# Layer norm and GELU: variance + eps and -mean/sigma of each tile computed on GpSimd instead of VectorE

## Chip, cores, metric

One core of one Trainium2 chip runs the kernel. The metric is device time in microseconds (us). The record calls a run slow when it is over 1.5% above the fastest of its kernel.

## The reference

```python
x: (8, 1024, 2048) float32; gamma, beta: (2048,); eps = 1e-5
mean = np.mean(x, axis=-1, keepdims=True)
var = np.var(x, axis=-1, keepdims=True)
out = gamma * (x - mean) / np.sqrt(var + eps) + beta
return 0.5 * out * (1 + np.tanh(np.sqrt(2 / np.pi) * (out + 0.044715 * out ** 3)))
```

## The kernel before

There are 8192 rows. A tile is 128 rows of 2048 columns; a batch is four tiles, moved by one load and one store of 4 MB. Five batch buffers are used in turn, and a load waits until the store from its buffer has landed. The last batch is cut into smaller pieces, so there are 65 tiles in all, and the stores are 15 large ones and a few small ones.

Each tile passes through four engines. VectorE takes statistics (four instructions of 512 columns and an aggregation) and adds eps to the variance. GpSimd computes (var + eps)^-0.5, which is 1/sigma; the text calls it the power. VectorE makes -mean/sigma of it. ScalarE scales (`yk = x/sigma - mean/sigma`, in bf16). VectorE multiplies by gamma (`zg`). TensorE adds beta and `zg` in PSUM. ScalarE applies GELU and, after each fourth tile, issues the store. In the code and the views, `sts` and `mvs` are the statistics and their aggregation (mean and variance), `ves` is variance + eps, `rss` 1/sigma and `nms` -mean/sigma. DVE stands for VectorE, ACT for ScalarE, POOL for GpSimd, PE for TensorE, and ACTq for what ScalarE's sequencer does itself, such as issuing a store. The parts that the change touches (`...` marks what is left out):

```python
            @block.gpsimd
            def _(po):
                ...
                def power(t, count):
                    c = slice(t % R, t % R + 1)
                    po.tensor_tensor(out=rss[:, c], in0=ves[:, c], in1=mhalf,
                                     op=ALU.pow)._wait_ge(s_a, count).then_inc(s_q, 1)
                ...
            @block.vector
            def _(ve):
                def mean(q, count):
                    c = slice(q, q + 1)
                    ve.tensor_scalar(out=nms[:, c], in0=mvs[:, q, 0:1], scalar1=rss[:, c], scalar2=-1.0,
                                     op0=ALU.mult, op1=ALU.mult)._wait_ge(s_q, count).then_inc(s_p, 1)

                def step(x, q, wait, count, before, count_q, count_n):
                    xr = x.rearrange("p (s f) -> p s f", f=FMAX)
                    for j in range(nsub):
                        ins = ve.bn_stats(out=sts[:, q, j, :], in_=xr[:, j, :])
                        if j == 0:
                            ...                               # the wait for the load
                            if before is not None:
                                mean(before, count_q)         # -mean/sigma of the tile before
                    ins.then_inc(s_o, 1)
                    ve.bn_aggr(out=mvs[:, q], in_=sts[:, q])._wait_ge(s_o, count + 1).then_inc(s_o, 1)
                    ve.tensor_scalar(out=ves[:, q:q + 1], in0=mvs[:, q, 1:2], scalar1=float(eps), scalar2=1.0,
                                     op0=ALU.add, op1=ALU.mult)._wait_ge(s_o, count + 2).then_inc(s_a, 1)
                    if count_n:
                        scale(before, count_n)

                def scale(q, count):                          # the gamma multiplication
                    ve.tensor_tensor(out=zgs[q % 2], in0=yks[q % 2], in1=g_t,
                                     op=ALU.mult)._wait_ge(s_n, count).then_inc(s_z, 1)
                ...
            @block.scalar
            def _(ac):
                ...
                for t in range(n_t + 1):
                    if t < n_t:
                        c = slice(t % R, t % R + 1)
                        ac.activation(out=yks[t % 2], in_=tiles[t], func=ACT.Identity, scale=rss[:, c],
                                      bias=nms[:, c])._wait_ge(s_p, t + 1).then_inc(s_n, 1)
                    i = t - 1
                    ...
                    ins = ac.activation(out=tiles[i], in_=pss[i % 2], func=ACT.Gelu_apprx_tanh)._wait_ge(s_t, i + 1)
                    ...                                       # the store, after each fourth tile
```

Of the kernel before, what the change touches and what calls it, by code (L numbers as in the profile page):

```python
# [8 lines left out]
ALU = mybir.AluOpType  # L9

R = 4
SLOTS = 5
# [6 lines left out]
def kernel(  # L19
# [41 lines left out]
    def sb(name, shape, dt):  # L61
        return pool.tile(shape, dt, name=name)

    xts = [sb(f"xt{s}", [P, R, d], f32) for s in range(SLOTS)]
# [11 lines left out]
    sts = sb("sts", [P, R, nsub, nc.vector.BN_STATS_DIM], f32)  # L76
    mvs = sb("mvs", [P, R, 2], f32)
    ves = sb("ves", [P, R], f32)
    rss = sb("rss", [P, R], f32)
    nms = sb("nms", [P, R], f32)  # L80

    def sem(name):
        return tc.alloc_semaphore(name)

    s_first = [sem(f"first{q}") for q in range(R)]
    s_tail = sem("tail")
    s_load_h = sem("load_h")
# [6 lines left out]
    s_o = sem("o")  # L94
    s_a = sem("a")
    s_z = sem("z")
    s_q = sem("q")
    s_p = sem("p")
# [7 lines left out]
    def slot(b):  # L106
        return (b + SLOTS - 1) % SLOTS

    def row(p):
        return rows[p:p + 1, :, :d // K]  # L110

    def split(v):
        return v.rearrange("o (k f) -> o k f", k=K)
# [11 lines left out]
    tiles = [xts[slot(b)][:, q] for b in range(B) for q in range(R)] + [xts[slot(B)][:, 0]]  # L125
    n_t = len(tiles)
# [9 lines left out]
    with tc.tile_critical(no_gpsimd_drain=True):  # L136
        with nc.Block(no_gpsimd_drain=True) as block:

            @block.sync
            def _(sy):  # L140
                for b in range(B):
                    s = slot(b)
                    if stored(b):
                        sy.wait_ge(s_store[s], stored(b))
                    for q in range(R):
                        if b == 0:
                            sy.dma_start(out=xts[s][:, q:q + 1], in_=xg[0, :, q:q + 1]).then_inc(s_first[q], 16)
                    if 0 < b < B - 1:
                        sy.dma_start(out=xts[s], in_=xg[b]).then_inc(s_load[s], 16)
                        if s == slot(B - 1):  # L150
                            sy.sem_inc(s_tail, 32)
                sy.dma_start(out=x_end[:, :R - 1], in_=last(xf)).then_inc(s_load[slot(B - 1)], 16)
                for v, a in x_half[:2]:
                    sy.dma_start(out=a, in_=v).then_inc(s_tail, 16)
                sy.wait_ge(s_store[slot(B)], stored(B))
                sy.dma_start(out=x_half[2][1], in_=x_half[2][0]).then_inc(s_load_h, 16)

            @block.gpsimd
            def _(po):
                po.memset(ones, 1.0)  # L160
                po.memset(ones_b, 1.0)
                po.memset(mhalf, -0.5)
                po.memset(ident, 0.0).then_inc(s_setp, 1)
                po.affine_select(out=ident, in_=ident, compare_op=ALU.not_equal, fill=1.0, base=0,  # L164
                                 pattern=[[-1, P]], channel_multiplier=1)._wait_ge(s_setp, 1).then_inc(s_setp, 1)

                def power(t, count):
                    c = slice(t % R, t % R + 1)
                    po.tensor_tensor(out=rss[:, c], in0=ves[:, c], in1=mhalf,  # L169
                                     op=ALU.pow)._wait_ge(s_a, count).then_inc(s_q, 1)  # L170

                with po.Fori(0, B):
                    for k in range(R):
                        power(k, k + 1)
                    po.sem_inc(s_a, -R)
                power(n_t - 1, 1)

            @block.vector
            def _(ve):
                def mean(q, count):  # L180

                    c = slice(q, q + 1)
                    ve.tensor_scalar(out=nms[:, c], in0=mvs[:, q, 0:1], scalar1=rss[:, c], scalar2=-1.0,  # L183
                                     op0=ALU.mult, op1=ALU.mult)._wait_ge(s_q, count).then_inc(s_p, 1)

                def step(x, q, wait, count, before, count_q, count_n):

                    xr = x.rearrange("p (s f) -> p s f", f=FMAX)
                    for j in range(nsub):
                        ins = ve.bn_stats(out=sts[:, q, j, :], in_=xr[:, j, :])  # L190
                        if j == 0:
                            if wait:
                                ins._wait_ge(*wait)
                                if wait[0] not in s_first:
                                    ins.then_inc(wait[0], -wait[1])
                            if before is not None:
                                mean(before, count_q)
                    ins.then_inc(s_o, 1)
                    ve.bn_aggr(out=mvs[:, q], in_=sts[:, q])._wait_ge(s_o, count + 1).then_inc(s_o, 1)  # L199
                    ve.tensor_scalar(out=ves[:, q:q + 1], in0=mvs[:, q, 1:2], scalar1=float(eps), scalar2=1.0,  # L200
                                     op0=ALU.add, op1=ALU.mult)._wait_ge(s_o, count + 2).then_inc(s_a, 1)
                    if count_n:
                        scale(before, count_n)

                def scale(q, count):
                    ve.tensor_tensor(out=zgs[q % 2], in0=yks[q % 2], in1=g_t,  # L206
                                     op=ALU.mult)._wait_ge(s_n, count).then_inc(s_z, 1)

                ve.memset(b_hl, 0.0).then_inc(s_m, 1)  # L209
                for q in range(R):  # L210
                    step(tiles[q], q, (s_first[q], 16), 2 * q, q - 1 if q else None, q, q)
                    if q == 0:

                        ve.tensor_tensor(out=split(b_hl[32:33]), in0=row(32), in1=split(b_hl[32:33]),  # L214
                                         op=ALU.subtract)._wait_ge(s_c, 2).then_inc(s_m, 1)
                        ve.wait_ge(s_c, 3)
                ve.sem_inc(s_o, -2 * R)
                ve.sem_inc(s_q, -(R - 1))
                ve.sem_inc(s_n, -(R - 1))
                with ve.Fori(0, (B - 1) // SLOTS):  # L220
                    for k in range(SLOTS * R):
                        s, q = divmod(k, R)
                        wait = (s_load[s], 16) if q == 0 else (s_tail, 32) if (s, q) == (slot(B - 1), R - 1) else None
                        step(xts[s][:, q], q, wait, 2 * k, (q - 1) % R, k + 1, k + 1)
                    ve.sem_inc(s_o, -2 * SLOTS * R)
                    ve.sem_inc(s_q, -SLOTS * R)
                    ve.sem_inc(s_n, -SLOTS * R)
                step(tiles[-1], 0, (s_load_h, 16), 0, R - 1, 1, 1)
                mean(0, 2)
                scale(0, 2)  # L230

            @block.scalar
# [104 lines left out]
```

## Time and profile before

| | before |
|---|---|
| time, median | 319.69 us (319.66 to 320.07) |
| busy: VectorE / ScalarE / TensorE / GpSimd | 269.2 / 257.7 / 248.0 / 79.5 us |
| the 16 DMA engines | 90% or more busy in 38 of 40 slices, 422 GB/s over the span |
| one store to the next, early / late | 16.69 / 19.36 us |

A busy share is an average over the whole span, so it can be high on an engine that bounds nothing. Three views are needed here: the slices (is anything busy all the time?), a table by stretch (does the same work take different times in different stretches?), and the waits (what did the busiest engine wait for when it did wait?). The prediction below shows the lines of all three.

### The profile page before, as it was taken

The page shows a single profiled execution, that of the slowest core. Times are in us where ns is not written, and L with a number is a line of the kernel's source. Part 1 is how long each engine was busy: PE and PEld are TensorE (multiplying, and loading weights), DVE is VectorE, ACT ScalarE, POOL GpSimd, SP SyncE. Part 2 cuts the span into 40 slices and gives each one's busy share as a digit, 9 for nine tenths or more (in the row PEclk, how much of TensorE's full clock was granted, in tenths as well). Part 3 has the DMA queues.
Part 4 walks back from the last instruction along what each step waited for, and adds up shares of the span by engine and source line. Part 5 has one row for each costly group of instructions (what it writes and reads, how often), then busy time and mean ns, then how long its engine had stood idle before and what let it go on. Part 6 is the DMA issues. An engine that isn't in the chain of part 4 may idle for free.

```text
span 317.9 us, 2115 instructions
## 1 busy us (share of the span) xinstructions
PE 248.0 (78%) x528; PEld 58.1 (18%) x528; DVE 269.2 (85%) x522; ACT 257.7 (81%) x134; POOL 79.5 (25%) x74
## 2 busy tenths in 40 slices
PE   2769988888888898888877868688685995898840
PEld 1211222111212122211211111121121121122100
DVE  3499999999999999999969789696996969999610
ACT  3579999999999999998969879697896959998850
POOL 1033323232323231323213212232213213221100
DMA  7999999999999999999999999999999999999994
GB/s 287 442 458 400 455 400 421 437 449 412 454 404 455 413 449 433 425 445 412 445 421 445 437 425 449 408 449 412 454 433 429 445 431 409 446 424 430 437 408 206
DMA packets 5753, 134.27 MB, mean 422 GB/s; under 512 B 710, under 2 KB 758, under 8 KB 758
## 3 DMA queue, kind: packets, MB, share of 16 engines
q1 hardware_dynamic: 2899, 67.11, 49.4%
q10 hardware_dynamic: 2851, 67.13, 49.0%
q14 instruction: 3, 0.02, 0.0%
HBM read 67.13 MB, written 67.11 MB: 422 GB/s over the span
## 4 chain that ended last, share of the span: by engine, by line
DMA 43%; DVE 27%; ACT 21%; PE 2%; issue 2%; ACTq 2%; DVEq 0%; SPq 0%
DMA out_dram<-xt 26%; DVE sts L190 15%; DMA xt<-in_x_dram 15%; ACT yk L246 13%; ACT xt L251 8%; DVE zg L206 8%; PE ps L269 2%; DMA rows<-in_gamma_dram 2%; DVE mvs L199 2%; ACTq L256 2%; DVE nms L183 1%; DVE ves L200 1%; ACT g_t L241 1%; ACTq L260 0%; DVEq L220 0%
## 5 line engine op out<-in xcount | busy, mean ns | idle before, releaser
L190 DVE BATCH_NORM_STATS2 sts<-xt 128x6 f32<-128x512 f32 x260 | 165.9, 679 | 22.1 <-DMA xt<-in_x_dram 19.8
L246 ACT ACTIVATE yk<-xt,nms,rss 128x2048 bf16<-128x2048 f32 x65 | 136.1, 2093 | 40.4 <-DVE nms L183 39.9
L286 PE MATMUL ps<-zg,ident 128*128 128x512 bf16 x260 | 122.7, 627 | 49.6 <-DVE zg L206 49.6
L169 POOL TENSOR_TENSOR rss<-ves,mhalf 128x1 f32<-128x1 f32 x65 | 78.5, 1208 | 218.5 <-DVE ves L200 159.0
L282 PE MATMUL ps<-b_hl,ones_b 33*128 33x512 bf16 x260 | 122.5, 624 | 2.2 <-PEq L277 2.2
L251 ACT ACTIVATE xt<-ps 128x2048 f32<-128x2048 f32 x65 | 120.6, 1856 | 1.6 <-PE ps L286 1.6
L206 DVE TENSOR_TENSOR zg<-yk,g_t 128x2048 bf16<-128x2048 bf16 x65 | 79.2, 1219 | 5.0 <-ACT yk L246 3.0
L286 PEld LDWEIGHTS ps<-zg,ident 128*128 128x128 bf16 x260 | 28.1, 130 | 144.2 <-DVE zg L206 108.4
L282 PEld LDWEIGHTS ps<-b_hl,ones_b 33*128 33x128 bf16 x260 | 27.5, 127 | 93.5 <-issue 89.8
L199 DVE BATCH_NORM_AGGREGATE mvs<-sts 128x2 f32<-128x24 f32 x65 | 17.1, 263 | 2.2
L183 DVE TENSOR_SCALAR nms<-mvs,rss 128x1 f32<-128x1 f32 x65 | 12.7, 196 | 0.0
L269 PE MATMUL ps<-rows,ones 1*128 1x512 f32 x8 | 7.2, 1076 | 6.1 <-DMA rows<-in_gamma_dram 6.1
L200 DVE TENSOR_SCALAR ves<-mvs 128x1 f32<-128x1 f32 x65 | 10.0, 153 | 2.2
L238 ACT ACTIVATE b_hl<-rows 1x2048 bf16<-1x2048 f32 x1 | 1.9, 1910 | 4.6 <-DMA rows<-in_beta_dram 4.6
L269 PEld LDWEIGHTS ps<-rows,ones 1*128 1x128 f32 x8 | 2.5, 325 | 9.2 <-DMA rows<-in_gamma_dram 6.1
L241 ACT ACTIVATE g_t<-ps 128x2048 bf16<-128x2048 f32 x1 | 1.9, 1877 | 2.6 <-PE ps L269 2.6
L214 DVE TENSOR_TENSOR b_hl<-rows,b_hl 1x2048 bf16<-1x2048 f32 x1 | 2.3, 2281 | 1.9 <-ACT b_hl L239 1.9
L234 ACT ACT_TABLE_LOAD x1 | 1.3, 1283 | 0.9 <-SPq L136 0.9
L209 DVE MEMSET b_hl<- 33x1024 uint32 x1 | 0.9, 912 | 1.2 <-SPq L136 1.2
L239 ACT ACTIVATE b_hl<-rows 1x2048 bf16<-1x2048 f32 x1 | 1.9, 1909 | 0.0
L160 POOL MEMSET ones<- 65x128 f32 x1 | 0.2, 201 | 0.5 <-SPq L136 0.5
L164 POOL TENSOR_SCALAR_AFFINE_SELECT ident<-ident 128x128 bf16<-128x128 bf16 x1 | 0.3, 292 | 0.1
(7 smaller groups left out, 0.9 us busy)
## 6 DMA issues: line engine op xcount, KB each, us to landing
out_dram<-xt ACTq DMA_DIRECT2D x15, 4096.0 KB, 35.0
xt<-in_x_dram SPq DMA_DIRECT2D x14, 4096.0 KB, 26.4
xt<-in_x_dram SPq DMA_DIRECT2D x4, 1024.0 KB, 8.2
xt<-in_x_dram SPq DMA_DIRECT2D x1, 3072.0 KB, 23.0
out_dram<-xt ACTq DMA_DIRECT2D x3, 1024.0 KB
xt<-in_x_dram SPq DMA_DIRECT2D x1, 512.0 KB, 21.4
out_dram<-xt ACTq DMA_DIRECT2D x1, 512.0 KB, 8.7
xt<-in_x_dram SPq DMA_DIRECT2D x1, 480.0 KB
```

The lines of the kernel that those rows point to most:

```text
L169: po.tensor_tensor(out=rss[:, c], in0=ves[:, c], in1=mhalf, op=ALU.pow)._wait_ge(s_a, count).then_inc(s_q, 1)
L183: ve.tensor_scalar(out=nms[:, c], in0=mvs[:, q, 0:1], scalar1=rss[:, c], scalar2=-1.0, op0=ALU.mult, op1=ALU.mult)._wait_ge(s_q, count).th ...
L190: ins = ve.bn_stats(out=sts[:, q, j, :], in_=xr[:, j, :])
L199: ve.bn_aggr(out=mvs[:, q], in_=sts[:, q])._wait_ge(s_o, count + 1).then_inc(s_o, 1)
L200: ve.tensor_scalar(out=ves[:, q:q + 1], in0=mvs[:, q, 1:2], scalar1=float(eps), scalar2=1.0, op0=ALU.add, op1=ALU.mult)._wait_ge(s_o, coun ...
L206: ve.tensor_tensor(out=zgs[q % 2], in0=yks[q % 2], in1=g_t, op=ALU.mult)._wait_ge(s_n, count).then_inc(s_z, 1)
L246: ac.activation(out=yks[t % 2], in_=tiles[t], func=ACT.Identity, scale=rss[:, c], bias=nms[:, c])._wait_ge(s_p, t + 1).then_inc(s_n, 1)
L251: ins = ac.activation(out=tiles[i], in_=pss[i % 2], func=ACT.Gelu_apprx_tanh)._wait_ge(s_t, i + 1)
L256: dma = ac.dma_start(out=v, in_=a)
L269: ins = pe.matmul(pss[0][:, cols(j)], lhsT=ones[64:65], rhs=rows[64:65, j * K // nsub:(j + 1) * K // nsub, :d // K], start=True, stop=True)
L282: ins = pe.matmul(ps[:, cols(j)], lhsT=ones_b, rhs=b_hl[:, cols(j)], start=True, stop=False)
L286: ins = pe.matmul(ps[:, cols(j)], lhsT=ident, rhs=zg[:, cols(j)], start=False, stop=True)
```

## The change

The intent: VectorE is the busiest engine, and -mean/sigma of a tile stood in VectorE's queue behind the first statistics of the next tile. GpSimd has both inputs and idles three quarters of the time, so it takes over both small instructions, and VectorE keeps six for each tile.

```diff
-                def power(t, count):
-                    c = slice(t % R, t % R + 1)
+                def small(t, k):
+                    q = t % R
+                    c = slice(q, q + 1)
+                    po.tensor_scalar(out=ves[:, c], in0=mvs[:, q, 1:2], scalar1=float(eps), scalar2=1.0,
+                                     op0=ALU.add, op1=ALU.mult)._wait_ge(s_a, k + 1).then_inc(s_q, 1)
                     po.tensor_tensor(out=rss[:, c], in0=ves[:, c], in1=mhalf,
-                                     op=ALU.pow)._wait_ge(s_a, count).then_inc(s_q, 1)
+                                     op=ALU.pow)._wait_ge(s_q, 2 * k + 1).then_inc(s_q, 1)
+                    po.tensor_scalar(out=nms[:, c], in0=mvs[:, q, 0:1], scalar1=rss[:, c], scalar2=-1.0,
+                                     op0=ALU.mult, op1=ALU.mult)._wait_ge(s_q, 2 * k + 2).then_inc(s_p, 1)
 ... (counts of the loop)
-                def mean(q, count):
-                    ... (the same instruction on VectorE)
 ...
-                            if before is not None:
-                                mean(before, count_q)
                     ins.then_inc(s_o, 1)
-                    ve.bn_aggr(out=mvs[:, q], in_=sts[:, q])._wait_ge(s_o, count + 1).then_inc(s_o, 1)
-                    ve.tensor_scalar(out=ves[:, q:q + 1], in0=mvs[:, q, 1:2], scalar1=float(eps), scalar2=1.0,
-                                     op0=ALU.add, op1=ALU.mult)._wait_ge(s_o, count + 2).then_inc(s_a, 1)
+                    ve.bn_aggr(out=mvs[:, q], in_=sts[:, q])._wait_ge(s_o, count + 1).then_inc(s_a, 1)
                     if count_n:
-                        scale(before, count_n)
+                        scale((q - 1) % R, count_n)
 ... (semaphore counts, calls)
```

More of the change, by code (lines that the diff above doesn't have):

```diff
@@ L165, in _, with step @@
                                  pattern=[[-1, P]], channel_multiplier=1)._wait_ge(s_setp, 1).then_inc(s_setp, 1)
-                def power(t, count):
-                    c = slice(t % R, t % R + 1)
+                def small(t, k):
[3 more added lines that the diff above has]
+                                     op0=ALU.add, op1=ALU.mult)._wait_ge(s_a, k + 1).then_inc(s_q, 1)
                     po.tensor_tensor(out=rss[:, c], in0=ves[:, c], in1=mhalf,
-                                     op=ALU.pow)._wait_ge(s_a, count).then_inc(s_q, 1)
+                                     op=ALU.pow)._wait_ge(s_q, 2 * k + 1).then_inc(s_q, 1)
+                    po.tensor_scalar(out=nms[:, c], in0=mvs[:, q, 0:1], scalar1=rss[:, c], scalar2=-1.0,
+                                     op0=ALU.mult, op1=ALU.mult)._wait_ge(s_q, 2 * k + 2).then_inc(s_p, 1)
                 with po.Fori(0, B):
                     for k in range(R):
-                        power(k, k + 1)
+                        small(k, k)
                     po.sem_inc(s_a, -R)
-                power(n_t - 1, 1)
+                    po.sem_inc(s_q, -2 * R)
+                small(n_t - 1, 0)
             @block.vector
             def _(ve):
-                def mean(q, count):
-                    c = slice(q, q + 1)
-                    ve.tensor_scalar(out=nms[:, c], in0=mvs[:, q, 0:1], scalar1=rss[:, c], scalar2=-1.0,
-                                     op0=ALU.mult, op1=ALU.mult)._wait_ge(s_q, count).then_inc(s_p, 1)
-                def step(x, q, wait, count, before, count_q, count_n):
+                def step(x, q, wait, count, count_n):
                     xr = x.rearrange("p (s f) -> p s f", f=FMAX)
@@ L190, in step @@
                         ins = ve.bn_stats(out=sts[:, q, j, :], in_=xr[:, j, :])
-                        if j == 0:
-                            if wait:
-                                ins._wait_ge(*wait)
-                                if wait[0] not in s_first:
-                                    ins.then_inc(wait[0], -wait[1])
-                            if before is not None:
-                                mean(before, count_q)
+                        if j == 0 and wait:
+                            ins._wait_ge(*wait)
+                            if wait[0] not in s_first:
+                                ins.then_inc(wait[0], -wait[1])
                     ins.then_inc(s_o, 1)
-                    ve.bn_aggr(out=mvs[:, q], in_=sts[:, q])._wait_ge(s_o, count + 1).then_inc(s_o, 1)
-                    ve.tensor_scalar(out=ves[:, q:q + 1], in0=mvs[:, q, 1:2], scalar1=float(eps), scalar2=1.0,
-                                     op0=ALU.add, op1=ALU.mult)._wait_ge(s_o, count + 2).then_inc(s_a, 1)
+                    ve.bn_aggr(out=mvs[:, q], in_=sts[:, q])._wait_ge(s_o, count + 1).then_inc(s_a, 1)
                     if count_n:
-                        scale(before, count_n)
+                        scale((q - 1) % R, count_n)
                 def scale(q, count):
@@ L210, in _ @@
                 for q in range(R):
-                    step(tiles[q], q, (s_first[q], 16), 2 * q, q - 1 if q else None, q, q)
+                    step(tiles[q], q, (s_first[q], 16), q, q)
                     if q == 0:
@@ L216, in _ @@
                         ve.wait_ge(s_c, 3)
-                ve.sem_inc(s_o, -2 * R)
-                ve.sem_inc(s_q, -(R - 1))
+                ve.sem_inc(s_o, -R)
                 ve.sem_inc(s_n, -(R - 1))
@@ L223, in _ @@
                         wait = (s_load[s], 16) if q == 0 else (s_tail, 32) if (s, q) == (slot(B - 1), R - 1) else None
-                        step(xts[s][:, q], q, wait, 2 * k, (q - 1) % R, k + 1, k + 1)
-                    ve.sem_inc(s_o, -2 * SLOTS * R)
-                    ve.sem_inc(s_q, -SLOTS * R)
+                        step(xts[s][:, q], q, wait, k, k + 1)
+                    ve.sem_inc(s_o, -SLOTS * R)
                     ve.sem_inc(s_n, -SLOTS * R)
-                step(tiles[-1], 0, (s_load_h, 16), 0, R - 1, 1, 1)
-                mean(0, 2)
+                step(tiles[-1], 0, (s_load_h, 16), 0, 1)
                 scale(0, 2)
```

## The prediction

> **What bounds the kernel now.** I read the page from the top: engine shares, the slices, the table of stretches, the waits, and last the order of time inside one tile. VectorE is the busiest engine by far, so at first sight six instructions per tile on it instead of eight ought to pay. The slices say otherwise.
>
> ```profile
> PE 248.0 (78%) x528; PEld 58.1 (18%) x528; DVE 269.2 (85%) x522; ACT 257.7 (81%) x134; POOL 79.5 (25%) x74
> DMA  7999999999999999999999999999999999999994
> HBM read 67.13 MB, written 67.11 MB: 422 GB/s over the span
> ```
>
> The DMA row is at 9 in every slice but the first and the last: the 16 DMA engines are never idle between some 3 us and the end. The 134.24 MB cannot be fewer (x is read once, the output written once). At 431 GB/s, which the table of stretches gives, they take 134.24/0.431 = 311.5 us. Before the first full microsecond of DMA lie about 2.5 us, behind the last about 4, so transfers alone explain a span of 318 us; the page says 317.9.
>
> ```profile
> 36.50:136.70 100.20, 88.90 (x194) 20.50 (x193) 97.83 (x194) 92.53 (x48) 29.58 (x24) 1.00 1.00 430
> 154.00:270.20 116.20, 88.94 (x194) 20.54 (x193) 98.41 (x194) 92.53 (x48) 29.58 (x24) 1.00 1.00 431
> ```
>
> These two stretches (columns: window, length, busy time of PE, PEld, DVE, ACT, POOL, clock, DMA share, GB/s) do the same work, six batches of four tiles. The first, from store to store, takes 100.2 us, 16.7 per batch or 4.17 per tile, and is paced by computing: five buffers were filled ahead. The second takes 116.2 us, 19.37 per batch or 4.84 per tile, and is paced by transfers: a batch moves 2 x 4.194 MB, and 8.389/19.37 is 433 GB/s. In both, DMA share is 1.00. In the first, stores only pile up behind the loads; in the second the arrears are paid. So a faster computing stage reaches the second stage sooner, and the sum of bytes is the same.
>
> ```profile
> DVE sts L190 <- DMA xt<-in_x_dram: 19.8, 9, 3.6
> ACT yk L246 <- DVE nms L183: 39.9, 64, 2.9
> SPq L149 <- DMA out_dram<-xt: 227.2, 10, 54.9
> ```
>
> The waits agree. VectorE's one large wait is for loads; the load queue waits 227 us for stores to clear buffers. The 39.9 us that ScalarE waits for -mean/sigma are what the change goes for.
>
> Now the loop inside one tile (start, duration, engine, line):
>
> ```profile
> 152.18 0.15 DVE L200 TENSOR_SCALAR ves<-mvs 128x1 f32<-128x1 f32 x1
> 152.25 1.22 DVE L206 TENSOR_TENSOR zg<-yk,g_t 128x2048 bf16<-128x2048 bf16 x1
> 152.41 1.47 POOL L169 TENSOR_TENSOR rss<-ves,mhalf 128x1 f32<-128x1 f32 x1 [2.66 <-DVE ves L200]
> 153.38 0.69 DVE L190 BATCH_NORM_STATS2 sts<-xt 128x6 f32<-128x512 f32 x1
> ...
> 153.98 0.20 DVE L183 TENSOR_SCALAR nms<-mvs,rss 128x1 f32<-128x1 f32 x1
> 154.10 1.87 DVE L190 BATCH_NORM_STATS2 sts<-xt 128x6 f32<-128x512 f32 x3
> ...
> 154.44 2.09 ACT L246 ACTIVATE yk<-xt,nms,rss 128x2048 bf16<-128x2048 f32 x1 [0.49 <-DVE nms L183]
> ```
>
> VectorE's gamma multiplication of tile t-1, the first statistics of t+1, and -mean/sigma of t stand in one queue; then ScalarE scales t, then VectorE multiplies t. The loop is 1.13 (multiplication to next issue) + 0.60 (statistics) + 0.15 (-mean/sigma to ScalarE) + 2.09 (scaling) + about 0.15 of hand-overs = 4.12 us. ScalarE's own work is 2.09 + 1.86 = 3.95, which is why it waits a quarter of a microsecond per tile.
>
> **What the Trainium skill says.** "SBUF — State Buffer", section "Who interferes with whom": a VectorE instruction with two SBUF inputs contends with a GpSimd instruction that reads SBUF, and the later one is blocked until the other is done. The trace agrees: GpSimd's power takes 0.55 us when it starts ahead of the multiplication and 1.46 (the median) when it starts behind it; above it ends at 153.88, 0.41 after the multiplication's end at 153.47. "Perfetto Trace Analysis", section "GPSIMD Engine Instruction", calls a GpSimd span unreliable and prefers start-to-start spacing; so I treat the GpSimd figures below as loose. "VectorE: DVE Perf Modes", section "Rules for kernel authors", advises to keep the number of VectorE instructions low; the trace agrees that small ones cost out of proportion: one element per partition takes 0.153 and 0.196 us. For bandwidth the SBUF page, section "A bandwidth-pool intuition that's wrong (but worth ruling out)", has 436 GB/s for DMA and SBUF but about 358 for HBM per core; the trace, at 431 to 433 with one core running, agrees with the first and not with the second.
>
> **The change, part by part.**
> Removed from VectorE: 65 x 0.196 = 12.7 us (-mean/sigma) and 65 x 0.153 = 10.0 us (variance + eps), 22.7 of 269.2; busy time should come to about 246.5 us, 78%. By starts, a tile costs 1.13 + 0.60 + 1.90 (three more statistics) + 0.28 (aggregation) = 3.91 instead of about 4.1 us of VectorE's queue.
>
> Added to GpSimd: two instructions per tile of 128x1. No such GpSimd instruction is in the trace; a memset of 128x1 takes 0.10 and the power 0.55 us, so my estimate is 0.3 each, and 0.1 for each hand-over (the power starts 0.09 after the instruction that it waits for in the case at 18.4 us). From aggregation to ScalarE, free of blocking: 0.1 + 0.3 + 0.1 + 0.55 + 0.1 + 0.3 + 0.1 = 1.55 us. But the multiplication starts right behind the aggregation, so one of the three will be held up. Before, this distance is 2.04 us (152.14 to 154.18).
>
> The new loop: let the multiplication of t-1 start d after the aggregation of t. The next aggregation ends d + 3.91 after that. With the distance L to -mean/sigma, scaling is over at L + 2.12. Both meet when d = L + 2.12 - 3.91 - d, so d = (L - 1.79)/2. If the power is the one held up, L = d + 1.21 (multiplication) + 0.42 (the rest of the power) + 0.5 = d + 2.13; that gives d = 0.34, L = 2.5, and 4.25 us per tile. Free of blocking it would be ScalarE's 3.97 to 4.05. So I expect 4.0 to 4.4 us per tile: the removed queue wait is largely replaced by GpSimd's chain. What matters is that all of this is below the 4.84 us per tile that transfers allow. L can grow to 3.7 us before it shows in the stretch paced by transfers.
>
> The end: the last large load lands at 278.15 and the last tile is done at 307.94. There each tile but one or two is paced by ScalarE, 2.09 + 1.77 + 0.34 for issuing a store + 0.14 = 4.34 us, so a loop of 4.25 hides. The longer L costs at most some 0.4 us once. Behind it lie transfers anyway: the last store of 512 KB, issued at 307.97, lands 8.7 us later, though its bytes need 0.524/0.431 = 1.2 us, and DMA is at full rate until 313. About 4 us of lateness at the end is hidden by stores that are queued already. Moved in the sum: 0 us, within what the order of reads and writes does to the rate.
>
> **Rivals.**
> First, **VectorE or the wait on it bounds**, and the gain arrives. For it speak 85% and the 39.9 us of ScalarE's wait; against it, DMA share 1.00 in both stretches. If it were so, the saving would be up to 22.7 us: 297 us.
> Second, **GpSimd's chain becomes the bound**: small GpSimd instructions of 1 us or more each, or all three blocked in turn by multiplications, or a hidden cost in switching between kinds of GpSimd instructions (the trace has 32 configuration records at the power's line, two per round of the loop, 5 to 11 ns each, with no visible delay). At 5.5 us per tile the time is an estimated 16 (before the first scaling) + 65 x 5.5 + 15 = 388 us. Against it: 0.55 us measured for the dearest of the three.
> Third, **a somewhat slower loop shows at the end only**: at 4.8 us per tile the last seven tiles would end 7 x 0.46 = 3.2 us later; the queued stores swallow nearly all, leaving 0 to 1 us, 320 to 321 us.
> Fourth, the rate itself moves with the mixture of loads and stores (425 to 444 GB/s between stretches); one part in 300 of it is 1 us, either way.
>
> **Range and chances.** The central case is unchanged, 319.7 us. The fourth rival gives about 1 us on either side, the third stretches the upper side: 318.7 to 321.0. Faster by over 2% (under 313.3) would need 134.24/305.1 = 440 GB/s in the mean, or fewer bytes: 0.02. Slower by over 2% (over 326) needs the second rival: 0.03. Within 2%: 0.95.
>
> **What would show it.** In the profile after: DMA row still 9 throughout and 421 to 424 GB/s over the span; VectorE's busy time near 246; stores some 19.4 us apart from the middle on; VectorE's waits for loads and for the scaled tile grown by about what it no longer does; the power shorter in the median, or the first of the three GpSimd instructions long instead; 4.0 to 4.4 us per tile in the early stretch. I am wrong on the loop if a tile there takes under 3.95 or over 4.5 us; wrong on the time if stores are over 19.6 us apart late, or DMA share falls below 0.97 before the last 10 us.

## The result and the profile after

The changed kernel took 320.0 us (median of 6 runs, 319.89 to 320.11), the kernel before 319.71 us in the same rounds. The ratio is 1.0006, with a 95% interval of 0.9993 to 1.0019: the same. A ratio here is the mean time of one kernel's fast runs over that of the other's of the same rounds, so it is not quite the ratio of the medians that are quoted.

The same lines of the page of the changed kernel (busy time by engine; the DMA row of the 40 slices; bytes):

```profile
PE 248.0 (78%) x528; PEld 58.1 (18%) x528; DVE 251.0 (79%) x392; ACT 255.4 (80%) x134; POOL 112.0 (35%) x204
DMA  7999999999999999999999999999999999999994
HBM read 67.13 MB, written 67.11 MB: 422 GB/s over the span
```

VectorE lost 18.2 us of busy time and 130 instructions, GpSimd gained 32.5 us, and the DMA row has not moved in a single digit. The table by stretch, again from store to store and for six batches each (columns as before: window, length, PE, PEld, DVE, ACT, POOL, clock, DMA share, GB/s):

```profile
36.00:134.30 98.30, 88.92 (x194) 20.53 (x193) 91.07 (x146) 91.25 (x48) 41.73 (x73) 1.00 1.00 429
153.00:269.20 116.20, 88.86 (x194) 20.49 (x192) 91.60 (x145) 91.89 (x48) 41.10 (x72) 1.00 1.00 432
```

The early stretch is 1.9 us shorter: 16.38 us per batch instead of 16.69, 4.095 per tile instead of 4.17. The late one has the same 116.2 us. Three lines of the waits (who waited for whom: us in total, times, longest) tell where VectorE's freed time went:

```profile
DVE sts L191 <- DMA xt<-in_x_dram: 24.6, 9, 3.7
DVE zg L202 <- ACT yk L239: 19.8, 34, 3.1
ACT yk L239 <- POOL nms L175: 36.7, 31, 3.0
```

Waits for loads went from 19.8 to 24.6 us, waits of the multiplication for the scaled tile from 3.0 to 19.8 us. ScalarE still waits 36.7 us for -mean/sigma, now from GpSimd.

How the new loop runs is to be read from the chain of waits in the early stretch (start, duration, what; the short pieces between are left out):

```profile
42.27 0.27 DVE mvs L197
...
42.63 1.04 POOL ves L171
...
43.74 0.55 POOL rss L173
...
44.39 0.28 POOL nms L175
...
44.69 2.10 ACT yk L239
...
46.82 1.23 DVE zg L202
48.05 2.40 DVE sts L191 x4
...
50.46 0.28 DVE mvs L197
```

From aggregation to aggregation, 42.27 to 50.46, are 8.19 us, but two tiles pass in it: the chain skips every second one. In the tile that the chain follows, the first GpSimd instruction takes 1.04 us. In the other tile the order of time shows that the third is the long one (start, duration, engine, line):

```profile
46.38 0.19 POOL L171 TENSOR_SCALAR ves<-mvs 128x1 f32<-128x1 f32 x1 [1.72 <-DVE mvs L197]
...
46.65 0.55 POOL L173 TENSOR_TENSOR rss<-ves,mhalf 128x1 f32<-128x1 f32 x1
...
46.82 1.23 DVE L202 TENSOR_TENSOR zg<-yk,g_t 128x2048 bf16<-128x2048 bf16 x1 [0.53 <-ACT yk L239]
47.31 0.87 POOL L175 TENSOR_SCALAR nms<-mvs,rss 128x1 f32<-128x1 f32 x1
```

The first GpSimd instruction took 1.03 to 1.04 us in the 31 tiles in which it started inside a gamma multiplication and 0.19 in the other 34; the third took 0.78 to 0.89 us in the 33 in which it started inside one and 0.27 in the other 32. There is no exception. The power, which always started outside, took 0.55 us each time.

### The profile page after: what moved, and what is told of

The parts are those of the page before. It is cut to its first block, busy times and chain, and to the rows that moved or that the text cites. A ratio compares the mean times of both kernels' runs of the same rounds, so it can differ in the third digit from the quotient of the medians.

```text
span 318.1 us, 2127 instructions
## 1 busy us (share of the span) xinstructions
PE 248.0 (78%) x528; PEld 58.1 (18%) x528; DVE 251.0 (79%) x392; ACT 255.4 (80%) x134; POOL 112.0 (35%) x204
## 4 chain that ended last, share of the span: by engine, by line
DMA 44%; ACT 19%; DVE 18%; POOL 9%; PE 2%; issue 2%; ACTq 1%; POOLq 0%; DVEq 0%; SPq 0%
DMA out_dram<-xt 27%; DMA xt<-in_x_dram 15%; ACT yk L239 14%; DVE sts L191 12%; POOL ves L171 5%; ACT xt L244 5%; DVE zg L202 5%; POOL rss L173 3%; PE ps L262 2%; DMA rows<-in_gamma_dram 2%; POOL nms L175 1%; DVE mvs L197 1%; ACTq L249 1%; ACT g_t L234 1%; POOLq L181 0%
## 5 line engine op out<-in xcount | busy, mean ns | idle before, releaser
L191 DVE BATCH_NORM_STATS2 sts<-xt 128x6 f32<-128x512 f32 x260 | 160.2, 678 | 26.5 <-DMA xt<-in_x_dram 24.6
L239 ACT ACTIVATE yk<-xt,nms,rss 128x2048 bf16<-128x2048 f32 x65 | 135.8, 2089 | 42.0 <-POOL nms L175 36.7
L171 POOL TENSOR_SCALAR ves<-mvs 128x1 f32<-128x1 f32 x65 | 38.6, 594 | 174.3 <-DVE mvs L197 174.3
L202 DVE TENSOR_TENSOR zg<-yk,g_t 128x2048 bf16<-128x2048 bf16 x65 | 77.6, 1194 | 19.8 <-ACT yk L239 19.8
L175 POOL TENSOR_SCALAR nms<-mvs,rss 128x1 f32<-128x1 f32 x65 | 36.6, 563 | 6.4
L173 POOL TENSOR_TENSOR rss<-ves,mhalf 128x1 f32<-128x1 f32 x65 | 35.8, 552 | 5.4
L197 DVE BATCH_NORM_AGGREGATE mvs<-sts 128x2 f32<-128x24 f32 x65 | 17.1, 264 | 2.2
```

What stands on the lines that cost most here:

```text
L171: po.tensor_scalar(out=ves[:, c], in0=mvs[:, q, 1:2], scalar1=float(eps), scalar2=1.0, op0=ALU.add, op1=ALU.mult)._wait_ge(s_a, k + 1).the ...
L173: po.tensor_tensor(out=rss[:, c], in0=ves[:, c], in1=mhalf, op=ALU.pow)._wait_ge(s_q, 2 * k + 1).then_inc(s_q, 1)
L175: po.tensor_scalar(out=nms[:, c], in0=mvs[:, q, 0:1], scalar1=rss[:, c], scalar2=-1.0, op0=ALU.mult, op1=ALU.mult)._wait_ge(s_q, 2 * k + 2 ...
L202: ve.tensor_tensor(out=zgs[q % 2], in0=yks[q % 2], in1=g_t, op=ALU.mult)._wait_ge(s_n, count).then_inc(s_z, 1)
```

## The experiments

Two questions are open after the result. Is it transfers that hide the faster computing stage, and how much could they hide? And is it the gamma multiplication that holds up GpSimd's instructions, and does that matter? Eleven kernels were run. "Half the stores" below means a wrong output: 15 large stores write only the first 1024 columns.

### Both kernels with half the stores

```diff
-    outs = {R * b + R - 1: [(og[b], xts[slot(b)], s_store[slot(b)])] for b in range(B - 1)}
+    outs = {R * b + R - 1: [(og[b][:, :, :d // 2], xts[slot(b)][:, :, :d // 2], s_store[slot(b)])] for b in range(B - 1)}
```

On the kernel before:

> The kernel before, with all stores but those of the last batch cut to the first half of the columns (wrong output on purpose): about 102 MB move instead of 134, 237 us at 431 GB/s, so transfers should no longer bound. Theory (transfers bound both kernels): the computing pace of the early stretch, 16.69 us per batch, now runs to the end: first store near 36.5, fifteenth near 36.5 + 14 x 16.69 = 270, five more tiles of 4.34 and the last store, about 297 us. Rival (something other than transfers, say VectorE, paces the late stretch): stores stay about 19.4 us apart from the middle on and the time near 320.

On the changed kernel:

> The changed kernel with the same half of the stores cut. Theory (the change makes the computing stage faster by 0.08 us per tile, 16.38 against 16.69 us per batch, and transfers hide it): about 36 + 14 x 16.38 = 265, the end as before, 292 to 293 us, 1.3 to 1.6% less than the kernel before with half its stores. Rival 1 (the whole 18 to 23 us that left VectorE would count if transfers did not bind): about 275 us. Rival 2 (the change is worth nothing in itself): equal to the kernel before with half its stores within 0.3%.

Measured: 300.36 us for the kernel before and 294.06 us for the changed one; against the unaltered kernel before in the same rounds the ratios are 0.9386 and 0.9188, so one against the other 0.9188/0.9386 = 0.979. The table by stretch over twelve batches, for the kernel before with half its stores and then for the changed one:

```profile
53.50:256.40 202.90, 177.82 (x386) 41.02 (x385) 195.66 (x385) 185.05 (x97) 59.13 (x48) 1.00 0.91 359
```

```profile
52.70:250.65 197.95, 177.83 (x386) 41.08 (x385) 182.11 (x290) 182.49 (x96) 84.80 (x145) 1.00 0.93 368
```

With less to move, the DMA share falls under 1 and the batches keep the computing pace to the end: 202.90/12 = 16.91 us and 197.95/12 = 16.50 us. So it is the transfers that hid the change, and the change in itself is worth 6.3 us, 2.1%, in kernels with half their stores. That is more than the 1.3 to 1.6% that I expected. Issuing a half-column store takes ScalarE's queue 0.55 us instead of 0.34; the kernel before pays all 0.21 per batch (16.69 to 16.90), the changed one pays 0.12 (16.38 to 16.50), presumably because ScalarE has some slack in its loop; that was not tested by itself. And it is far less than the 18.2 us of busy time that left VectorE: without the transfers, a loop across three engines is the limit, not VectorE's queue.

### More work in GpSimd's chain: how much can be hidden?

Further powers, each waiting for the one before, lengthen the loop without touching transfers or VectorE:

```diff
+                    for e in range(2):
+                        po.tensor_tensor(out=spare[:, c], in0=ves[:, c], in1=mhalf,
+                                         op=ALU.pow)._wait_ge(s_q, 4 * k + 2 + e).then_inc(s_q, 1)
```

Two more:

> The changed kernel with all its stores and two more powers in GpSimd's chain for each tile, each waiting for the one before it (result unused). The loop of two tiles holds one chain, so 2 x 0.65 us more in it should give (8.19 + 1.3)/2 = 4.75 us per tile in the early stretch, 19.0 us per batch, just under the 19.37 that transfers take. Theory (transfers bound): time 320 to 322 us although computing is 16% slower. Rival (the computing loop is on the path all along): 65 x 0.65 = 42 us more, near 362 us.

Three more:

> The changed kernel with three more powers in GpSimd's chain for each tile. Early pace by the loop of two tiles: (8.19 + 3 x 0.65)/2 = 5.07 us per tile, 20.3 us per batch, over the 19.37 that transfers take. Theory (the limit is 4.84 us per tile): now the chain shows, stores 20.3 us apart to the end, DMA share under 1, about 36 + 14 x 20.3 + 26 + 6 = 350 us. Rival (the limit lies elsewhere, much higher): still 320 us.

Measured: 331.92 us with two (ratio 1.0373, interval 1.0356 to 1.0391) and 356.19 us with three (one look). The paces came near what was expected, 18.87 and 20.39 us per batch (19.0 and 20.3): a loop of two tiles with one chain of GpSimd's in it. With three more powers it is no longer quite the same loop: the held instruction in its chain is the power (1.53 us at 69.25), where with two it is still the first (1.04 at 65.27). The time did not come as expected: with two, 18.87 is below the 19.36 of the late batches, and yet 12 us came on top. ScalarE's store issues in the run with two show it (start, duration, queue, line):

```profile
283.79 0.34 ACTq L253 DMA_DIRECT2D out_dram<-xt  x1
302.66 0.34 ACTq L253 DMA_DIRECT2D out_dram<-xt  x1
...
325.64 0.59 ACTq L253 DMA_DIRECT2D out_dram<-xt  x1
```

The fifteenth large store goes out at 302.66 instead of 287.09, the very last at 325.64, and the end of the run follows 6.3 us later (in the kernel before 319.69 - 307.97 = 11.7 us later, because other stores are still queued). The pace of the late batches was the wrong yardstick: in the kernel before only six of the fourteen steps between large stores take 19.36 us; the first six take 16.7. The mean of all fourteen is (287.09 - 36.47)/14 = 17.9 us. What has to be compared is two sums: all transfers, 320 us; and all computing, that is first store + 14 batches + 21 to 23 us for the last five tiles + about 6.3 us. For the run with two that is 38.48 + 14 x 18.87 + 22.98 + 6.3 = 331.9 us; as the 6.3 is taken from this run, the sum only restates it. Two more runs tested it, with one more power, and with one more power and one more variance + eps:

> The changed kernel with one more power in GpSimd's chain. The run with two had 18.87 us per batch and took 332 us, against what I had expected, so the limit of 19.37 us per batch was wrong. New theory: what counts is the whole computing time, first store + 14 batches + about 22 for the last five tiles + 6.3 to the end, against the 320 us of the transfers. Here a batch should take (8.19 + 0.62)/2 x 4 = 17.6 us and the sum is 37.2 + 247 + 22 + 6.3 = 312: still hidden, 319.5 to 320.5 us, though computing is 5.6% slower than in the kernel before. Rival (anything added over the pace of the kernel before is paid in part): 14 x 0.9 = 13 us more, 333.

> The changed kernel with one more power and one more variance + eps in GpSimd's chain: (8.19 + 0.62 + 0.27)/2 x 4 = 18.15 us per batch. By the new theory the sum is 37.7 + 254 + 22.5 + 6.3 = 320.5: this is the edge, 320 to 322.5 us. By the limit of 19.37 us per batch that I had predicted it would be 320 exactly as without; by the rival that all is paid, about 340.

Measured: 320.49 us (ratio 1.0013, interval 0.9985 to 1.0042) and 322.07 us (1.0062, interval 1.0033 to 1.009). With one more power a batch takes 17.63 us, 0.9 us more than in the kernel before, and nothing clear of noise shows in the time. Its store issues show the hand-over from one limit to the other:

```profile
195.91 0.34 ACTq L253 DMA_DIRECT2D out_dram<-xt  x1
213.53 0.34 ACTq L253 DMA_DIRECT2D out_dram<-xt  x1
231.58 0.34 ACTq L253 DMA_DIRECT2D out_dram<-xt  x1
251.47 0.34 ACTq L253 DMA_DIRECT2D out_dram<-xt  x1
```

Steps of 17.62 us, then 18.05, then 19.89: computing sets the pace until about 213 us, where it had been until about 137 us in the kernel before; from there transfers do. The second run never reaches that: 18.28 us per batch to the end, the last store at 315.78, the end 6.3 us after it. Its 322.07 us are within 2% of the kernel before, but the interval leaves out 1, so here computing has begun to show. The edge lies between 17.63 and 18.28 us per batch.

### Where the held instructions come from

A memset of -mean/sigma to 0 in place of the third GpSimd instruction writes the same column and reads nothing:

```diff
-                    po.tensor_scalar(out=nms[:, c], in0=mvs[:, q, 0:1], scalar1=rss[:, c], scalar2=-1.0,
-                                     op0=ALU.mult, op1=ALU.mult)._wait_ge(s_q, 2 * k + 2).then_inc(s_p, 1)
+                    po.memset(nms[:, c], 0.0)._wait_ge(s_q, 2 * k + 2).then_inc(s_p, 1)
```

> The changed kernel with the third GpSimd instruction replaced by a memset of -mean/sigma to 0 at the same place with the same wait (wrong result on purpose): it writes and reads nothing. Theory (only GpSimd's reads are held up by the multiplication): the memset takes 0.1 to 0.2 us also where it falls beside a multiplication, where the instruction that it replaces took 0.79 to 0.88, while the first instruction still takes 1.03 in some tiles. Rival (any GpSimd instruction is held up): about 0.8 us there. Time 320 in either case.

Measured: 319.87 us (one look), 16.27 us per batch early. From the order of time:

```profile
38.53 1.22 DVE L201 TENSOR_TENSOR zg<-yk,g_t 128x2048 bf16<-128x2048 bf16 x1 [0.47 <-ACT yk L238]
39.02 0.10 POOL L175 MEMSET nms<- 128x1 f32 x1
```

The memset stands in the middle of a multiplication and takes 0.10 us, in all of the 17 tiles in which it started inside one, while in the same run the first instruction took 1.03 to 1.24 us inside one (31 tiles) and the power 1.58 to 1.60 (16 tiles). The span of an instruction that reads nothing might be doubted, but the trace also records when semaphores are raised: the memset's at 39.13 us, while the multiplication runs until 39.75. In the changed kernel the third instruction in the same place raised it at 40.00, after the multiplication's end at 39.86. What is held up is reading, as the theory had it.

### The multiplication moved away from GpSimd's instructions

```diff
                     for j in range(nsub):
                         ins = ve.bn_stats(out=sts[:, q, j, :], in_=xr[:, j, :])
                         ...
+                        if j == 1 and count_n:
+                            scale((q - 2) % R, count_n)
                     ...
-                    if count_n:
-                        scale((q - 1) % R, count_n)
```

With half the stores, so that computing shows:

> The changed kernel with half the stores, and VectorE's gamma multiplication of a tile moved behind the second statistics of the next tile but one, so that GpSimd's three instructions run beside instructions with one input only. Theory (in the changed kernel every second tile's chain is held up by about 0.85 us[...]): first and third GpSimd instruction short in every tile (0.19 and 0.27 us), 3.9 us per tile, 15.6 to 15.8 us per batch, bound by ScalarE, time 281 to 287 us. Rival (the long GpSimd spans are an artefact of the records or come from elsewhere): spans stay long in some tiles and a batch stays at 16.4 us, time 292 or more.

With all stores:

> The changed kernel with all its stores and the multiplication behind the second statistics of the next tile but one. Theory (transfers bound): early batches near 15.7 us, late ones still 19.37, time 319.5 to 321.0, the same within 0.4%, though computing is 6% faster than in the kernel before. Rival (computing paces the end, or each store's moment does): up to 7 tiles x 0.2 = 1.4 us less, or, since a tile's end comes later behind a load, 1 to 2 us more.

Measured: 284.72 us with half the stores (0.8898 of the kernel before, so 0.8898/0.9188 = 0.968 of the changed kernel with half its stores), 319.84 us with all of them (ratio 0.9993, interval 0.9977 to 1.001). With all stores the two stretches read (four early batches, seven late ones):

```profile
35.70:98.10 62.40, 59.59 (x130) 13.71 (x130) 60.34 (x97) 60.39 (x33) 28.58 (x48) 1.00 1.00 424
135.10:270.60 135.50, 103.69 (x225) 23.90 (x224) 106.03 (x169) 107.10 (x56) 42.70 (x84) 1.00 1.00 432
```

15.6 us per batch early, the best of all kernels here, 19.36 late as ever, and the same time. My reason for it was half wrong, though. With half the stores the third GpSimd instruction (durations min, median, max in ns) did not get short in most tiles (44 of 65 took 1.30 us):

```profile
L175 POOL TENSOR_SCALAR nms<-mvs,rss x65: 264/1304/1306, 9.5 to 268.6; 128x1 f32<-128x1 f32 x65
```

The multiplication now starts about 1.05 us after the end of the aggregation, and so just beside the third instruction, which starts 1.0 us after it and is held for all of it; the first is 0.19 us in every tile. The batches became shorter all the same. My reading is that the multiplication now waits a statistics pair longer for its tile, so the held chain has the time. What was won is that the chain no longer lies on the loop: in the whole run with all stores, where 36 third instructions are held, ScalarE waits for GpSimd once (us in total, times, longest), at the head, and the changed kernel has 31 such waits with 36.7 us.

```profile
ACT yk L240 <- POOL nms L175: 3.1, 1, 3.1
```

So the hold-up is real, and its removal was not what this run tested.

### One part of the change at a time

-mean/sigma alone on GpSimd:

> Only one part of the change: -mean/sigma on GpSimd, variance + eps still on VectorE. The power should be the instruction held up (about 1.46 us), the third about 0.27; distance from aggregation to ScalarE about 0.04 + 0.15 + 0.09 + 1.46 + 0.1 + 0.27 = 2.1 us, as in the changed kernel's held tiles; VectorE's queue costs 0.15 us more per tile. Early pace 4.05 to 4.2 us per tile, if the -mean/sigma instruction's place in VectorE's queue was the whole of the old wait; time 320. Rival (moving variance + eps is what shortened the loop): early pace stays 4.17.

Variance + eps alone on GpSimd:

> The other part of the change alone: variance + eps on GpSimd, -mean/sigma still in VectorE's queue behind the first statistics. The first GpSimd instruction should be the one held up by the multiplication in nearly every tile (about 1.03 us), the power 0.55. -mean/sigma can then start 0.1 + 1.03 + 0.07 + 0.55 + 0.08 = 1.83 us after the aggregation, where VectorE reaches it after 1.13 + 0.60 = 1.73: nothing won, 4.12 to 4.2 us per tile, 16.6 to 16.9 us per batch. Rival (moving variance + eps is what shortens the loop, since moving -mean/sigma alone left 16.65): 16.3 to 16.4. Time 320 either way.

Measured (one look each): 320.15 us and 320.03 us; early batches 16.65 us with -mean/sigma moved alone and 17.10 to 17.30 us with variance + eps moved alone, against 16.69 before and 16.38 with both. The parts don't add up. Variance + eps alone makes the loop slower, beyond my range of 16.6 to 16.9: its chain from the early stretch reads

```profile
65.44 1.27 POOL ves L170
...
66.79 0.56 POOL rss L172
...
67.38 0.21 DVE nms L187
67.59 1.80 DVE sts L194 x3
```

GpSimd's held instruction (1.26 us where I had expected 1.03) and the power end after VectorE has reached -mean/sigma, so now VectorE's queue, with three statistics behind it, stands and waits for GpSimd. -mean/sigma alone leaves the power held (1.45 to 1.62 us in 47 tiles; in 17 the third instruction was held too, 0.87 to 0.91, against my expectation) and wins 0.04 us per batch. Only with both is VectorE's queue free of GpSimd's results while the hold lies on the loop in every second tile only.

## Why the prediction was right, and where it was not

- **Transfers bound the kernel, and the change moves nothing**: right, and shown. DMA row and late stretch are the same to the digit; with half the stores both kernels become faster and differ by 6.3 us.
- **The old loop, 4.12 us**: the sum is right for three tiles in four. The fourth, where ScalarE issues a store ahead of the scaling, takes 4.32 us, and the tile that the prediction shows is such a one: from the start of -mean/sigma to the scaling it has 0.46 us (154.44 - 153.98), not the 0.15 of the sum; the other tiles have 0.23, with 0.06 for the hand-over after the scaling instead of 0.15. The 2.04 us "from aggregation to ScalarE" end at -mean/sigma; to the scaling it is 2.29 there and 2.07 in most tiles.
- **The new loop, 4.0 to 4.4 us per tile, most likely 4.25**: 4.095 measured, within the range, but with steps behind it that failed, so that it fell there is in part luck. One is the held instruction: the equation took the power, which was never held in the changed kernel (0.55 us in all 65 tiles). The other is that of one delay d for every tile. The loop alternates instead: after a held first instruction (multiplication right behind the aggregation) comes a tile whose multiplication is 0.53 us late, which lets the first instruction and the power through and holds the third, with time to spare. The equation has one value for what in fact takes turns. The sizes put in were fair: 0.19 and 0.27 us for the two instructions instead of 0.3 each.
- **VectorE's busy time near 246 us**: 251.0. The step subtracted the sum of durations, 22.7 us, but busy time counts overlapping instructions once. All of VectorE's durations fell by 24.6 us (298.9 to 274.3); 6.4 of it had run beside another of its instructions, as -mean/sigma did beside statistics and variance + eps beside the multiplication, so 18.2 are left.
- **"L can grow to 3.7 us before it shows", from 4.84 us per tile**: wrong, and the wrong mechanism that a reader should note, though the time did not depend on it. 4.72 us per tile cost 12 us. The sum over the whole run decides, and its edge lies between 17.63 and 18.28 us per batch, 4.41 and 4.57 per tile. The expected 4.25 and even the 4.4 at the end of the range lie below that edge, so the verdict holds by the right yardstick too. The third rival, 4.8 us per tile for 320 to 321 us, fell with it.
- **The end up to 0.4 us later**: the last store went out at 307.24 instead of 307.97, 0.7 us earlier, and was worth nothing; it landed 9.6 us after its issue instead of 8.7, behind queued stores. That the queue swallows lateness was right.
- **Where VectorE's freed time goes**: right. Waits for loads grew by 4.8 us and for the scaled tile by 16.8, together 21.6 us. VectorE's idle time in all (span less busy time) grew by 18.4 us, from 48.7 to 67.1; other gaps shrank by the difference.

The 0.3 us between the two medians lies within the interval and is not explained.

## What to carry to other kernels

When the DMA row is full from end to end, work that is taken from the busiest engine turns into waits of that engine; test it by halving the bytes, which shows what the change is worth in itself. To know how much slower computing may become, compare the whole sum of computing, head and tail included, with the whole sum of transfers, not the pace of one stretch with that of another. A cheap instruction moved to an idle engine is cheap only if the result is no longer waited for in a queue with other work, so moving half of a chain can be worse than moving none (here 17.1 to 17.3 us per batch against 16.69, hidden by transfers).

## What the Trainium skill lacked or had wrong

- "GPSIMD Engine Reference", section "Performance versus the Vector engine", has figures for 2048 and 512 elements per partition, and none for a single one. For one element per partition the runs show 0.10 us for a memset, 0.19 for variance + eps, 0.27 for -mean/sigma with its per-partition operand, 0.55 for the power, and 0.07 to 0.11 us from one to the next through a semaphore.
- "SBUF — State Buffer", section "Who interferes with whom", is confirmed for GpSimd behind VectorE: reading instructions are held (0.19 becomes 1.03, 0.27 becomes 0.78 to 0.89, 0.55 becomes 1.46), a memset is not (0.10 in 17 of 17). It says that issue order decides who blocks, so a multiplication should be blocked behind a running power; that is not seen here. The multiplications that started beside one took 1.224 to 1.226 us in all 33 cases (at 46.82, for example, the power running from 46.65 to 47.20), and the single one of the run with no GpSimd instruction beside it took 1.225.
- The same page's 358 GB/s for HBM per core (section "A bandwidth-pool intuition that's wrong (but worth ruling out)") is half of a stack's rate, and the row does not say that one core running alone gets more: 429 to 432 GB/s in the stretches of both kernels. The skill as a whole does not lack this: "HBM Reference", section "Specifications (TRN2)", has about 425 GB/s for a core alone.
- "Perfetto Trace Analysis", section "GPSIMD Engine Instruction", calls GpSimd's spans unreliable and says that they do not compose. Here they do: a power recorded with 0.55 us and 0.08 us to the next instruction have a start-to-start spacing of 0.63 us, and each further power made the loop of two tiles 0.62 us longer ((18.87 - 16.38)/4). Only the recorded order is loose: in the run with the multiplication moved, third instructions recorded 0.04 to 0.05 us ahead of it were held for the whole of it (1.30 us).
